# Convolution taps on one engine, tokens and context together, and two modulation groups in another stage

## The chip, the cores and the metric
The kernel runs on one core of a Trainium2 chip. The metric is the device time of one execution in microseconds. TensorE (PE) multiplies matrices, VectorE (DVE), ScalarE (ACT) and GpSimd (POOL) work on tiles of 128 partitions, and SyncE (SP) issues most transfers. Each engine executes its own queue of instructions in order.

## The reference
Two transformer blocks run one after the other on 512 tokens of width 1024 and, in the first block, 256 context tokens. The first block has two layers (`l` = 0 and 1). What matters for the change:

```python
def conformer_conv(u, conv_w, conv_b, ln_g, ln_b):
    a, gate = jnp.split(u, 2, axis=-1)
    h = a * jax.nn.sigmoid(gate)
    half = C_CONV_WIDTH // 2                       # C_CONV_WIDTH = 31
    h = lax.conv_general_dilated(h, conv_w[:, None, :], window_strides=(1,), padding=((half, half),),
                                 dimension_numbers=('NWC', 'WIO', 'NWC'),
                                 feature_group_count=C_CHANNELS) + conv_b   # C_CHANNELS = 256
    return jax.nn.silu(layer_norm(h, ln_g, ln_b))

# per layer: six modulation vectors of 1024 from the condition c (and from c_ctx for the context)
m = jax.nn.silu(cond) @ w_mod_l[:, :n_chunks * D_MODEL] + b_mod_l[:n_chunks * D_MODEL]
h = modulate(x, sh1, sc1)          # layer_norm(x) * (1 + sc1) + sh1
u = h @ w_in_l                     # queries, keys, values of attentions A and B, the convolution's 512 columns
x = layer_norm(DEEPNORM_ALPHA * x + g1 * o, ...)       # o: attentions and convolution through w_out
h2 = modulate(x, sh2, sc2)
x = layer_norm(DEEPNORM_ALPHA * x + g2 * ec_moe(h2, ...), ...)   # 16 experts
```

In layer 0 the convolution runs on the tokens and, apart from them, on the context; in layer 1 on the tokens alone. Only the shift and scale of the first LayerNorm (`sh1`, `sc1`) are needed before the projections; `g1`, `sh2`, `sc2` and `g2` are needed behind the attention.

## The kernel before
The stages follow one another: in layer 0 the LayerNorm and first modulation (to some 40 us), the projections with the convolution (to 245), attention (to 408), the output projection and router (to 500), the experts (to 1130); then layer 1 with its two LayerNorms (to 1190), projections (to 1313), attention (to 1420), output projection and experts; then the second block.

**Projections.** `gemm(j)` (L418) makes one of 16 chunks of 128 columns. The activations are split into `hi` and `lo` (HH, HL) and the weights into `wh` (cast on ACT, L300) and `wl` (the difference, L288, on DVE), so that three matmuls per k (128 rows) keep the precision; all matmuls go through the helper `mm`, L98. `px` holds 512 tokens, `pc` 256 context tokens. `wh` and `wl` have two buffers each: the cast for chunk j+2 waits for the last matmul of chunk j, and `wl` stands behind that in DVE's queue. Chunks 0 to 3 give the convolution's input `hp` (L492), 4 to 6 the keys, which `ksplit` (L444 to L451) splits through one buffer `kf` (filled by ACT, L459 and L460), 7 to 12 the queries, 13 to 15 the values. Chunk 4 and the queries of A are rotated (`rope`: a matmul into `rot`, `t` on DVE L439, `qf` times `cos` on POOL L440, the sum L441).

**Convolution.** For each of two groups of 128 channels, `hp` holds the tokens with 15 zeros on either side and behind them the context with its own zeros (`segs`). Tap 0 is a product plus bias on POOL (L504). The token taps are one DVE instruction each (L510), acc = hp shifted by t, times cw[t], plus acc, over 128x512. The context taps take two POOL instructions each over 128x256: a product into `cvt` (L516) and an addition to `acc` (L517). In layer 1, which has no context, the last 12 taps of each channel group go to POOL in the same manner over 128x512 (L520 to L524, `POOL_TAPS`), into an accumulator that DVE adds (L525). `taps(n)` issues the next n DVE taps between projections, and `conv_out` ends the convolution with LayerNorm and SiLU.

**Modulation.** `mod_group(l, g)` (L152) computes two of layer l's six vectors for both conditions: eight k-steps, each a load of 1 MB of `w_mod` through a ring of four buffers that the projection weights share (`load`, L144, issued by SP in order), and four matmuls with the columns `sT`; then a bias addition on DVE (`bm`, L160), a write of `ms` to memory, four transposes (L166) and copies into `modT` (L169). `mods` chains groups, and `next(mods)` advances by one k-step. Layer 0's projections work off (0,1) and (0,2), one step per `gemm`; layer 0's attention works off (1,0), (1,1) and (1,2), one step per unit. Layer 1 has none. `sT` is used again by the router (L753).

A scheduler of the language's compiler settles the order on each engine by its own estimates; `keep_in_program_order` pins a few instructions, so moving or resizing one instruction reorders its neighbours.

Of the kernel before, what the change touches and what calls it, by code (L numbers as in the profile page):

```python
# [10 lines left out]
F32 = mybir.dt.float32  # L11
# [3 lines left out]
AF = mybir.ActivationFunctionType  # L15
OP = mybir.AluOpType
# [4 lines left out]
P = 128  # L21
# [7 lines left out]
NEG = -1.0e30  # L29
RING = 4  # L30
MRING = (7, 9)
POOL_TAPS = (0, 12)
RIGHT = (1, 3)


# [26 lines left out]
class K:  # L62
# [38 lines left out]
    def setup(self):  # L101
        nc, A = self.nc, self.A
        self.cp = self.pool(self.es, "consts")
        self.ringp = self.pool(self.es, "ring", bufs=RING)
        self.dr = self.pool(self.es, "scratch", space=DRAM)
        self.ident = self.t(self.cp, [P, P], tag="ident")
        nc.scalar.dma_start(self.ident, A["ident"])
        self.nh8 = self.t(self.cp, [P, 8], tag="nh8")
        nc.gpsimd.memset(self.nh8, -0.5)
        self.nhalf = self.nh8[:, 0:1]  # L110
        cT = self.t(self.cp, [P, KC, 2], tag="cT")
        nc.scalar.dma_start(cT, A["cT"])
        self.sT = self.t(self.cp, [P, KC, 32], tag="sT")
        nc.gpsimd.memset(self.sT, 0.0)
        th = self.t(self.cp, [P, KC, 2], tag="cth")
        nc.scalar.activation(th, cT, AF.Tanh, scale=0.5)
        nc.vector.tensor_scalar_mul(cT, cT, 0.5)
        nc.vector.scalar_tensor_tensor(out=self.sT[:, :, 0:2], in0=th, scalar=1.0, in1=cT, op0=OP.add, op1=OP.mult)
        self.lnc = self.t(self.cp, [P, KC], tag="lnc")
        nc.gpsimd.dma_start(self.lnc, A["ln1_T"])  # L120
        self.xsum = [self.t(self.cp, [P, 1], tag=f"xsum{t}") for t in range(6)]
        self.modT = [self.t(self.cp, [P, 2, 48], tag=f"modT{l}") for l in range(2)]
        self.ms = {}

    def pipeline(self, units):

# [107 lines left out]
    def layer(self, l):  # L234
        nc, A, es = self.nc, self.A, ExitStack()
        last = l == 1
        NT = 4 if last else 6
        W = 512 if last else 768
# [15 lines left out]
        cw = self.t(kvp, [P, 2, 31], tag="cw")  # L254
# [3 lines left out]
        cb, cg5, cb5 = vec[:, 0, :], vec[:, 1, :], vec[:, 2, :]  # L258
# [18 lines left out]
        ps = self.pool(ea, f"psa{l}", bufs=2, space=PSUM)  # L277
# [8 lines left out]
        def low(j, eng):  # L286
            wt, wh, wl = nw[j]
            return eng.tensor_tensor(out=wl, in0=wt, in1=wh.bitcast(F32), op=OP.subtract)  # L288

        def weights(j, ahead=False):  # L290
            if j % 2 == 0:
                self.wt = self.load(A["w_in_t"][l, j // 2].rearrange("p k f -> p (k f)")).rearrange("p (k f) -> p k f", k=KC)
            wt = self.wt[:, :, (j % 2) * P : (j % 2) * P + P]
            if j in (2, 3):

                wh, wl = (kb[:, o * D : (o + 1) * D].rearrange("p (k f) -> p k f", k=KC) for o in (2 * j - 4, 2 * j - 3))
            else:
# [10 lines left out]
        if l == 0:  # L308

            zT = QA + QB + [vz[:, 0:768], vz[:, 768:1536]]  # L310
            for t in range(6):
                self.ln(XN[:, t, :], XN[:, t, :], small)
                for k0 in (0, 4):
                    tp = self.t(ps, [P, 4, P], tag="tr")
# [15 lines left out]
        else:  # L330

            gb = self.ring().rearrange("p (i d) -> p i d", i=2)
            for i in range(2):
                nc.sync.dma_start(gb[:, i], A["ln_vec"][l - 1, 2 + i : 3 + i, :].broadcast_to([P, D]))
            pin = self.tc.keep_in_program_order
            weights(0, ahead=True)
            weights(1, ahead=True)
            weights(2, ahead=True)
# [58 lines left out]
        ev = ExitStack()  # L397
        cvp = ev.enter_context(self.tc.tile_pool(name=f"conv{l}", bufs=1, side="right", reuse_waits="tile"))
        hp = [self.t(cvp, [P, W + (30 if last else 60)], tag=f"hp{c}") for c in range(2)]
        acc = [self.t(cvp, [P, W], tag=f"acc{c}") for c in range(2)]  # L400
        for c in range(2):
            nc.gpsimd.memset(hp[c][:, 0:15], 0.0)
            nc.gpsimd.memset(hp[c][:, 527:542], 0.0)
# [4 lines left out]
        wkp = self.pool(ea, f"wk{l}", bufs=2)  # L408
# [4 lines left out]
        nc.sync.dma_start(cos, A["cosA"])  # L413
        nc.sync.dma_start(sin, A["sinA"])

        mods = self.mods([(0, 1), (0, 2)] if l == 0 else [], ps, "mod", wkp, 1)

        def gemm(j, need_c):  # L418
            if len(nw) <= j:
# [63 lines left out]
        segs = [(0, 512, 15)] + ([] if last else [(512, 256, 557)])  # L483
        for c in range(2):
            px, pc = gemm(2 * c, not last)
            th = self.t(wkp, [P, 768], tag="kf", bufs=1)
# [6 lines left out]
        tap = []  # L493
# [4 lines left out]
            del tap[:n]  # L498

        def conv(c):  # L500
            for a, n, o in segs:
                o -= 15
                dst = acc[c][:, a : a + n]
                nc.gpsimd.tensor_scalar(dst, hp[c][:, o : o + n], cw[:, c, 0:1], cb[:, c : c + 1], op0=OP.mult, op1=OP.add)  # L504

                n0 = 31 if a else 31 - POOL_TAPS[l]
                for t in range(1, n0):
                    if a == 0:
                        tap.append(
                            lambda dst=dst, o=o, n=n, t=t: nc.vector.scalar_tensor_tensor(  # L510
                                out=dst, in0=hp[c][:, o + t : o + t + n], scalar=cw[:, c, t : t + 1], in1=dst, op0=OP.mult, op1=OP.add
                            )
                        )
                    else:
                        tmp = self.t(wkp, [P, 256], tag="cvt", bufs=4)
                        nc.gpsimd.tensor_scalar(tmp, hp[c][:, o + t : o + t + n], cw[:, c, t : t + 1], 0.0, op0=OP.mult, op1=OP.add)  # L516
                        nc.gpsimd.tensor_tensor(out=dst, in0=dst, in1=tmp, op=OP.add)  # L517
                if n0 < 31:
                    dst2 = self.t(cvp, [P, n], tag=f"acc2{c}")
                    for t in range(n0, 31):  # L520
                        tmp = dst2 if t == n0 else self.t(cvp, [P, n], tag="cvt2", bufs=2)
                        nc.gpsimd.tensor_scalar(tmp, hp[c][:, o + t : o + t + n], cw[:, c, t : t + 1], 0.0, op0=OP.mult, op1=OP.add)
                        if t > n0:
                            nc.gpsimd.tensor_tensor(out=dst2, in0=dst2, in1=tmp, op=OP.add)  # L524
                    tap.append(lambda dst=dst, dst2=dst2: nc.vector.tensor_tensor(dst, dst, dst2, op=OP.add))  # L525

        def conv_out():
            for t0, t1 in ((0, 4), (4, NT)):
                if t1 == t0:
                    continue  # L530
                zz = []
                for t in range(t0, t1):
                    tp = self.t(ps, [P, 512], tag="tr")
                    for c in range(2):
                        nc.tensor.transpose(tp[:, c * P : (c + 1) * P], acc[c][:, t * P : (t + 1) * P], self.ident)
                    mv, rs = self.ln_stats(tp, small, 256)
                    z = self.t(wkp, [P, 256], tag="cvt", bufs=4)
                    nc.vector.tensor_scalar(z, tp[:, 0:256], mv[:, 0:1], rs, op0=OP.subtract, op1=OP.mult)
                    zz.append(z)
                n, q0 = (t1 - t0) * P, t0 * P  # L540
                for c in range(2):
                    tp = self.t(ps, [P, 512], tag="tr")
                    for i, z in enumerate(zz):
                        nc.tensor.transpose(tp[:, i * P : (i + 1) * P], z[:, c * P : (c + 1) * P], self.ident)
                    u = self.t(wkp, [P, 512], tag="qf")
                    th = self.t(wkp, [P, 512], tag="t2")
                    nc.scalar.activation(u[:, :n], tp[:, :n], AF.Identity, bias=cb5[:, c : c + 1], scale=cg5[:, c : c + 1])
                    nc.scalar.activation(th[:, :n], u[:, :n], AF.Tanh)
                    nc.vector.scalar_tensor_tensor(out=acc[c][:, q0 : q0 + n], in0=th[:, :n], scalar=1.0, in1=u[:, :n], op0=OP.add, op1=OP.mult)

        for c in range(2):
            conv(c)
# [24 lines left out]
        MH = self.t(mixp, [P, KC, 768], F32R, tag="hi")  # L577
        ML = self.t(mixp, [P, KC, 768], F32R, tag="lo")
        self.MH, self.ML = MH, ML
        for c in range(2):  # L580
            nc.scalar.copy(MH[:, 6 + c, 0:W], acc[c])
            nc.vector.tensor_tensor(ML[:, 6 + c, 0:W], acc[c], MH[:, 6 + c, 0:W].bitcast(F32), op=OP.subtract)
        ea.close()
        ev.close()

# [2 lines left out]
        ap_ = self.pool(eb, f"at{l}", bufs=2)  # L588
        sm = self.pool(eb, f"ats{l}", bufs=4)
        ps = self.pool(eb, f"psb{l}", bufs=2, space=PSUM)  # L590
# [149 lines left out]
        ps = self.pool(ec, f"psc{l}", bufs=2, space=PSUM)  # L740
# [1246 lines left out]
```

## Time and profile before
| | us |
|---|---|
| median of 3 runs | 2653.32 (2651.34 to 2657.65) |
| profiled execution, its own time | 2650.53 |
| its span, first to last instruction | 2648.4 |
| TensorE busy | 2442.7 (92%) |
| VectorE / ScalarE / GpSimd busy | 1204.3 / 707.6 / 579.5 |
| mean granted TensorE clock | 0.964 |

The span leaves out 2.1 us around the first and the last instruction. Busy shares are means over stages with very different limits, so the rows below look at stages: how busy each engine is in a stretch of time, what an engine waited for, and single instructions in order of time. [...]

### The profile page before, as it was taken

How to read it: one execution, taken by the hardware profiler on the slowest of the kernel's cores; microseconds unless marked ns; L12 is line 12 of the kernel's file. 1: busy time of each engine (PE TensorE's matmuls, PEld its weight loads, DVE VectorE, ACT ScalarE, POOL GpSimd, SP SyncE). 2: the span in 40 equal slices, each digit the busy share in tenths (PEclk: the TensorE clock that was granted, in tenths of full speed). 3: DMA queues.
4: the chain of work that ended last, by engine and by line, in shares of the span. 5: the costliest groups of instructions: out<-in, count | busy, mean ns of one | idle time of the engine just before them, and what ended most of it. 6: DMA issues, size and time to landing. Idle time of an engine off the chain costs nothing. (4 is left out here: it accounts for less than half of the span.)

```text
span 2648.4 us, 37078 instructions
## 1 busy us (share of the span) xinstructions
PE 2442.7 (92%) x14946; PEld 1471.4 (56%) x14946; DVE 1204.3 (45%) x2478; ACT 707.6 (27%) x1404; POOL 579.5 (22%) x747
## 2 busy tenths in 40 slices
PE   6779999899999999957999699999989999999999
PEld 3566677533333333246787443333337878888887
DVE  6874675612222222379586412221138577432332
ACT  3023562210111110142364210000014357222321
POOL 4971350100000000069242100000005234111100
PEclk9989999899999999978999799999999999999999
DMA  8235804599999888530202699999992311222320
GB/s 341 95 119 211 301 22 152 207 358 409 352 335 340 337 328 334 207 125 32 80 25 105 244 419 420 420 419 420 420 395 84 125 49 52 85 96 80 112 96 32
DMA packets 141436, 581.42 MB, mean 220 GB/s; under 512 B 11985, under 2 KB 13009, under 8 KB 125649
## 3 DMA queue, kind: packets, MB, share of 16 engines
q1 hardware_dynamic: 132368, 549.62, 53.8%
q0 software_dynamic: 5152, 18.88, 1.9%
q10 hardware_dynamic: 3744, 10.56, 1.0%
q8 instruction: 117, 1.92, 0.3%
q14 instruction: 55, 0.44, 0.1%
HBM read 568.54 MB, written 10.49 MB: 219 GB/s over the span
## 5 line engine op out<-in xcount | busy, mean ns | idle before, releaser
L98 PE MATMUL mm<-m,xt 128*32 128x512 f32 (+1 forms) x2536 | 403.9, 594 | 0.0
L98 PEld LDWEIGHTS mm<-m,xt 128*32 128x32 f32 (+1 forms) x2536 | 119.3, 115 | 211.5 <-issue 205.0
L98 PE MATMUL mm<-r,xt 128*32 128x512 f32 (+1 forms) x1128 | 232.5, 595 | 0.0
L1153 DVE TENSOR_TENSOR xn<-xn,tr 128x512 f32<-128x512 f32 x120 | 78.4, 685 | 249.3 <-PE tr L98 249.3
L98 PE MATMUL mm<-m,hT 128*32 128x512 f32 (+1 forms) x792 | 179.8, 597 | 6.0 <-DMA m<-w_down 6.0
L978 POOL DMA_INDIRECT gat<-zd,ip x24 | 22.9, 954 | 623.1 <-PE tr L986 583.5
L98 PE MATMUL mm<-mr,xt 128*32 128x512 f32 (+1 forms) x432 | 131.4, 605 | 1.5 <-DVE xt L991 1.2
L510 DVE SCALAR_TENSOR_TENSOR acc<-hp,cw,acc 128x512 f32<-128x512 f32 x96 | 123.3, 1300 | 10.2 <-POOL acc L504 8.4
L98 PE MATMUL mm<-r,hT 128*32 128x512 f32 (+1 forms) x560 | 125.5, 597 | 1.9 <-DMA r<-w_down 1.9
L1120 DVE SCALAR_TENSOR_TENSOR yf<-mm,gp,g 128x512 f32<-128x512 f32 x32 | 24.0, 751 | 223.1 <-PE mm L98 221.4
L98 PEld LDWEIGHTS mm<-r,xt 128*32 128x32 f32 (+1 forms) x1128 | 67.4, 117 | 88.3 <-issue 83.5
L98 PE MATMUL px<-hi,wh 128*128 128x512 f32 x224 | 95.3, 431 | 18.9 <-ACT kf L459 17.2
L98 PE MATMUL px<-hi,wl 128*128 128x512 f32 x224 | 93.6, 418 | 20.5 <-DVE wl L288 20.5
L640 POOL TENSOR_SCALAR p<-p,rl 128x768 f32<-128x768 f32 (+2 forms) x96 | 79.1, 828 | 133.1 <-DVE rl L639 94.7
L98 PEld LDWEIGHTS mm<-m,hT 128*32 128x32 f32 (+1 forms) x792 | 52.9, 121 | 94.8 <-issue 73.6
L98 PE MATMUL pv<-ptT,VN 128*64 128x128 f32 x1360 | 95.4, 284 | 6.5 <-DVE lo L622 5.5
L98 PE MATMUL px<-HH,uh 128*128 128x512 f32 x256 | 99.9, 391 | 0.7 <-ACT HH L1777 0.7
L98 PE MATMUL po<-dl,rh 128*128 128x512 f32 x256 | 99.2, 390 | 1.4 <-DVE dl L1207 1.4
L98 PE MATMUL px<-HH,ul 128*128 128x512 f32 x256 | 99.9, 390 | 0.0
L98 PE MATMUL px<-HL,uh 128*128 128x512 f32 x256 | 99.9, 390 | 0.0
L98 PE MATMUL po<-dh,rh 128*128 128x512 f32 x256 | 98.9, 390 | 0.0
L98 PE MATMUL po<-dh,rl 128*128 128x512 f32 x256 | 98.6, 390 | 0.0
(523 smaller groups left out, 5326.1 us busy)
## 6 DMA issues: line engine op xcount, KB each, us to landing
m<-w_gate SPq DMA_DIRECT2D x79, 1024.0 KB, 14.6
m<-w_down SPq DMA_DIRECT2D x71, 1024.0 KB, 17.8
m<-w_up SPq DMA_DIRECT2D x62, 1024.0 KB, 9.5
r<-w_mod SPq DMA_DIRECT2D x48, 1024.0 KB, 6.4
r<-w_down SPq DMA_DIRECT2D x41, 1024.0 KB, 9.4
r<-w_up SPq DMA_DIRECT2D x40, 1024.0 KB, 17.8
r<-w_gate SPq DMA_DIRECT2D x31, 1024.0 KB, 13.2
mr<-w_up SPq DMA_DIRECT2D x20, 1024.0 KB, 5.2
```

The lines of the kernel that those rows point to most:

```text
L98: return self.nc.tensor.matmul(out, lhsT, rhs, start=start, stop=stop)
L510: lambda dst=dst, o=o, n=n, t=t: nc.vector.scalar_tensor_tensor(out=dst, in0=hp[c][:, o + t : o + t + n], scalar=cw[:, c, t : t + 1], in1= ...
L640: nc.gpsimd.tensor_scalar(p[:, :n], p[:, :n], rl, 0.0, op0=OP.mult, op1=OP.add)
L978: nc.gpsimd.indirect_dma_start(out=g[0:n], out_offset=None, in_=self.zd[l][s], in_offset=bass.IndirectOffsetOnAxis(ap=self.route[s][2][0:n ...
L1120: nc.vector.scalar_tensor_tensor(out=y, in0=d, scalar=gp[:, p : p + 1], in1=G2[0][:, c], op0=OP.mult, op1=OP.mult)
L1153: nc.vector.tensor_tensor(dst, dst, so, op=OP.add)
```

## The change
All 31 taps are computed without POOL. Tap 0 (product and bias) is an ACT instruction; the other 30 of each channel group are DVE instructions. In layer 0 one instruction covers tokens and context: `hp` is read over 798 = 512 + 30 + 256 elements, and `acc` has 30 unused columns between tokens and context (the context begins at `A0` = 542). Layer 1 has 60 DVE taps of 512 instead of 36 and two additions. The normalised values `z` use `hp`'s space in place of `cvt`, and the split of the convolution's result into MH and ML is made in one piece for tokens and one for context. The groups (1,1) and (1,2) move from layer 0's attention into layer 1's projections, so each layer's projections carry (l,1) and (l,2), and layer 0's attention carries (1,0) alone. As `sT` has been overwritten by then, `set_s` fills it again before layer 1.

```diff
-POOL_TAPS = (0, 12)
...
+    def set_s(self):
+        nc, (th, cT) = self.nc, self.silu
+        nc.gpsimd.memset(self.sT, 0.0)
+        nc.vector.scalar_tensor_tensor(out=self.sT[:, :, 0:2], in0=th, scalar=1.0, in1=cT, op0=OP.add, op1=OP.mult)
...
             pin = self.tc.keep_in_program_order
+            self.set_s()
             weights(0, ahead=True)
...
-        acc = [self.t(cvp, [P, W], tag=f"acc{c}") for c in range(2)]
+        acc = [self.t(cvp, [P, W if last else W + 30], tag=f"acc{c}") for c in range(2)]
+        A0 = 542
...
-        mods = self.mods([(0, 1), (0, 2)] if l == 0 else [], ps, "mod", wkp, 1)
+        mods = self.mods([(l, 1), (l, 2)], ps, "mod", wkp, 1)
...
         def conv(c):
-            for a, n, o in segs:
-                o -= 15
-                dst = acc[c][:, a : a + n]
-                nc.gpsimd.tensor_scalar(dst, hp[c][:, o : o + n], cw[:, c, 0:1], cb[:, c : c + 1], op0=OP.mult, op1=OP.add)
-                n0 = 31 if a else 31 - POOL_TAPS[l]
...
+            dst = acc[c]
+            n = dst.shape[1]
+            nc.scalar.activation(dst, hp[c][:, 0:n], AF.Identity, bias=cb[:, c : c + 1], scale=cw[:, c, 0:1])
+            for t in range(1, 31):
+                tap.append(
+                    lambda t=t: nc.vector.scalar_tensor_tensor(
+                        out=dst, in0=hp[c][:, t : t + n], scalar=cw[:, c, t : t + 1], in1=dst, op0=OP.mult, op1=OP.add
+                    )
+                )
...
-                    z = self.t(wkp, [P, 256], tag="cvt", bufs=4)
+                    z = hp[t % 2][:, t // 2 * 256 : t // 2 * 256 + 256]
...
         for c in range(2):
-            nc.scalar.copy(MH[:, 6 + c, 0:W], acc[c])
-            nc.vector.tensor_tensor(ML[:, 6 + c, 0:W], acc[c], MH[:, 6 + c, 0:W].bitcast(F32), op=OP.subtract)
+            for (a, n, o), q0 in zip(segs, (0, A0)):
+                nc.scalar.copy(MH[:, 6 + c, a : a + n], acc[c][:, q0 : q0 + n])
+                nc.vector.tensor_tensor(ML[:, 6 + c, a : a + n], acc[c][:, q0 : q0 + n], MH[:, 6 + c, a : a + n].bitcast(F32), op=OP.subtract)
...
-        mods = self.mods([(1, 0), (1, 1), (1, 2)] if l == 0 else [], ps, "mod", ap_, 1)
+        mods = self.mods([(1, 0)] if l == 0 else [], ps, "mod", ap_, 1)
```

The order of VectorE's queue in layer 0, from the first taps to the rotation of chunk 4, before. `hp_95` is the input of the second channel group, `wl_1058` the low half of chunk 6's weights:

```order
L510 SCALAR_TENSOR_TENSOR acc_96_433<-hp_94_431,cw_124,acc_96_433 128x512 x18
L492 SCALAR_TENSOR_TENSOR hp_95_432<-kf_632,px_643 128x512
L492 SCALAR_TENSOR_TENSOR hp_95_432<-kf_632,pc_644 128x256
L510 SCALAR_TENSOR_TENSOR acc_96_433<-hp_94_431,cw_124,acc_96_433 128x512 x3
L510 SCALAR_TENSOR_TENSOR acc_97_434<-hp_95_432,cw_124,acc_97_434 128x512
...
L288 TENSOR_TENSOR wl_1058<-r_1055,wh_1057 128x1024
...
L439 TENSOR_TENSOR t_189_956<-rot_954,sin_449 128x512
```

The same place in the changed kernel, where the same product is `wl_876`:

```order
L514 SCALAR_TENSOR_TENSOR acc_96_433<-hp_94_431,cw_124,acc_96_433 128x798 x13
L500 SCALAR_TENSOR_TENSOR hp_95_432<-kf_632,px_643 128x512
L500 SCALAR_TENSOR_TENSOR hp_95_432<-kf_632,pc_644 128x256
L514 SCALAR_TENSOR_TENSOR acc_96_433<-hp_94_431,cw_124,acc_96_433 128x798 x2
L514 SCALAR_TENSOR_TENSOR acc_97_434<-hp_95_432,cw_124,acc_97_434 128x798
...
L293 TENSOR_TENSOR wl_876<-r_873,wh_875 128x1024
...
L447 TENSOR_TENSOR t_129_774<-rot_772,sin_449 128x512
```

Taps of 798 elements stand in place of those of 512, and fewer of them ahead of each product: 13 instead of 18 ahead of the second `hp`, and counted from the first tap, 23 instead of 32 ahead of this `wl` and 31, 37, 41, 46 and 53 ahead of the next five (42, 46, 53 and twice 60 before).

PE's queue at the beginning of layer 1 in the changed kernel, from the last product of the experts to the transposes of the second LayerNorm (`VN`, `z`; `r` is a ring buffer with `w_mod`):

```order
L97 MATMUL tr_8553<-yc_1595_8509,oh_1592_8501 128x512
L97 MATMUL mod_8897<-r_8898,sT_69 32x512 x4
L97 MATMUL mod_8897<-r_8931,sT_69 32x512 x4
L97 MATMUL mod_8897<-r_8963,sT_69 32x512 x4
L375 MATMUL tr_8707<-ident_63,VN_8573 128x128
L375 MATMUL tr_8716<-ident_63,VN_8573 128x128
...
L97 MATMUL mod_8897<-r_8996,sT_69 32x512 x4
L375 MATMUL tr_8707<-ident_63,z_1666_8703 128x128
```

Before, the first of these transposes followed the last product of the experts at once. The other four steps of this group now stand among the remaining transposes and the first projections, and the second group's eight among the later projections.

SP's queue for the same stage in the changed kernel (the first two loads of `w_in_t`, the bias, band and table loads are left out; `x2d` is a write of the residual):

```order
L149 DMA r_8898<-w_mod 128x2048
L149 DMA r_8931<-w_mod 128x2048
...
L362 DMA x2d_92<-xn_3798 128x1024
L149 DMA r_8963<-w_mod 128x2048
...
L149 DMA r_9388<-w_mod 128x2048
L149 DMA r_9435<-w_in_t 128x2048
...
L168 DMA ms_1766_9338<-bm_8895 128x512
L157 DMA bm_9385<-bmr 128x512
L149 DMA r_9441<-w_mod 128x2048
```

Before, this queue held eight loads of `w_in_t` and no `w_mod`, `bm` or `ms`. Now loads of `w_mod` alternate with those of `w_in_t`, the third waits its turn behind the first `x2d`, and the second group's loads stand behind the write of `ms`.

## Rows read from the trace of the kernel before
**Rows 1.** The page, part 1: busy us, share of the span, instructions.
```profile
PE 2442.7 (92%) x14946; PEld 1471.4 (56%) x14946; DVE 1204.3 (45%) x2478; ACT 707.6 (27%) x1404; POOL 579.5 (22%) x747
```
**Rows 2.** Four stretches: length, busy PE, PEld, DVE, ACT, POOL, clock, DMA share, GB/s.
```profile
100.00:180.00 80.00, 50.51 (x254) 39.25 (x252) 79.45 (x57) 16.74 (x24) 77.23 (x89) 0.83 0.21 74
...
245.00:340.00 95.00, 88.13 (x726) 55.55 (x728) 66.50 (x204) 54.06 (x121) 35.22 (x52) 0.99 0.81 304
...
1190.00:1250.00 60.00, 46.86 (x195) 37.71 (x194) 59.17 (x49) 14.79 (x21) 59.45 (x42) 0.89 0.07 21
...
1320.00:1410.00 90.00, 84.25 (x822) 74.48 (x823) 74.21 (x209) 63.03 (x143) 45.24 (x77) 0.96 0.06 18
```
**Rows 3.** Waits, 60 to 225 us: engine, line, releaser: us, times, longest.
```profile
PE px L98 <- DVE wl L288: 13.0, 3, 10.8
...
PE px L98 <- ACT kf L459: 8.9, 1, 8.9
...
PE mod L166 <- DVE bm L160: 6.1, 1, 6.1
```
**Rows 4.** Stretches of 10 us in layer 0's projections.
```profile
110.00:120.00 10.00, 3.75 (x11) 3.22 (x12) 10.00 (x6) 0.00 (x0) 10.00 (x13) 0.51 0.01 2
...
130.00:140.00 10.00, 3.99 (x12) 3.48 (x13) 9.94 (x8) 4.82 (x7) 10.00 (x10) 0.53 0.20 55
...
150.00:160.00 10.00, 6.99 (x29) 6.14 (x30) 9.94 (x8) 2.65 (x4) 10.00 (x12) 0.66 0.17 54
```
**Rows 5.** Groups by shape, DVE, 0 to 420 us: busy us, mean ns | idle before.
```profile
L510 DVE SCALAR_TENSOR_TENSOR acc<-hp,cw,acc 128x512 f32<-128x512 f32 x60 | 76.8, 1300 | 8.5 <-POOL acc L504 7.4
...
L288 DVE TENSOR_TENSOR wl<-r,wh 128x1024 fp32r<-128x1024 f32 x14 | 21.4, 1544 | 8.0 <-ACT wh L300 8.0
```
**Rows 6.** Timeline of DVE: start us, duration us (layer 0; the last row layer 1).
```profile
67.81 17.55 DVE L510 SCALAR_TENSOR_TENSOR acc<-hp,cw,acc 128x512 f32<-128x512 f32 x18
...
130.84 0.73 DVE L510 SCALAR_TENSOR_TENSOR acc<-hp,cw,acc 128x512 f32<-128x512 f32 x1
...
135.87 1.21 DVE L288 TENSOR_TENSOR wl<-r,wh 128x1024 fp32r<-128x1024 f32 x1
...
1135.79 1.28 DVE L353 SCALAR_TENSOR_TENSOR xn<-xn,rs,r 128x1024 f32<-128x1024 f32 x1
```
**Rows 7.** Timeline of ACT: the casts behind projections 4, 9, 10 and 11.
```profile
92.72 1.05 ACT L300 CAST wh<-r 128x1024 fp32r<-128x1024 f32 x1 [18.22 <-PE pc L98]
...
177.03 1.05 ACT L300 CAST wh<-r 128x1024 fp32r<-128x1024 f32 x1 [11.18 <-PE pc L98]
...
188.46 1.05 ACT L300 CAST wh<-r 128x1024 fp32r<-128x1024 f32 x1 [9.61 <-PE pc L98]
...
198.96 1.05 ACT L300 CAST wh<-r 128x1024 fp32r<-128x1024 f32 x1 [8.68 <-PE pc L98]
```
**Rows 8.** Timeline of PE: one k-step of a modulation group.
```profile
103.47 1.07 PE L98 MATMUL mod<-r,sT 128*32 128x512 f32 x8
```
**Rows 9.** The tile `mod`, PE, 245 to 345 us: passes and waits.
```profile
L98 PE MATMUL mod<-r,sT x192: 590/592/617, 246.8 to 329.5; 128*32 128x512 f32 x192
...
  DMA r<-w_mod: 3.1, 2
```
**Rows 10.** Timeline, layer 1: PE's first transposes; SP's writes of `x2d`.
```profile
1144.23 0.69 PE L369 MATMUL tr<-ident,VN 128*128 128x128 f32 x2 [10.53 <-DVE VN L362]
...
1137.11 9.94 SPq L356 DMA_DIRECT2D x2d<-xn  x4
```
**Rows 11.** The page, part 6: loads of `w_mod`, KB each, us to landing.
```profile
r<-w_mod SPq DMA_DIRECT2D x48, 1024.0 KB, 6.4
```
**Rows 12.** Waits, 1120 to 1310 us (layer 1).
```profile
PE px L98 <- ACT kf L459: 8.3, 2, 7.1
...
PE px L98 <- DVE wl L288: 7.5, 2, 4.9
```
**Rows 13.** Groups by shape, DVE, 1120 to 1310 us.
```profile
L510 DVE SCALAR_TENSOR_TENSOR acc<-hp,cw,acc 128x512 f32<-128x512 f32 x36 | 46.5, 1300 | 1.7 <-POOL acc L504 1.0
```

More of the change, by code (lines that the diff above doesn't have):

```diff
@@ L113, in setup @@
         self.sT = self.t(self.cp, [P, KC, 32], tag="sT")
-        nc.gpsimd.memset(self.sT, 0.0)
         th = self.t(self.cp, [P, KC, 2], tag="cth")
@@ L117, in setup @@
         nc.vector.tensor_scalar_mul(cT, cT, 0.5)
-        nc.vector.scalar_tensor_tensor(out=self.sT[:, :, 0:2], in0=th, scalar=1.0, in1=cT, op0=OP.add, op1=OP.mult)
+        self.silu = th, cT
+        self.set_s()
         self.lnc = self.t(self.cp, [P, KC], tag="lnc")
@@ L335, in layer @@
             pin = self.tc.keep_in_program_order
+            self.set_s()
             weights(0, ahead=True)
@@ L500, in conv @@
         def conv(c):
-            for a, n, o in segs:
-                o -= 15
-                dst = acc[c][:, a : a + n]
-                nc.gpsimd.tensor_scalar(dst, hp[c][:, o : o + n], cw[:, c, 0:1], cb[:, c : c + 1], op0=OP.mult, op1=OP.add)
-                n0 = 31 if a else 31 - POOL_TAPS[l]
[L507 to L525, printed above, removed]
+            dst = acc[c]
[7 more added lines that the diff above has]
+                )
         def conv_out():
@@ L531, in conv_out @@
                 zz = []
+                n, q0 = (t1 - t0) * P, (A0 if t0 else 0)
                 for t in range(t0, t1):
@@ L534, in conv_out @@
                     for c in range(2):
-                        nc.tensor.transpose(tp[:, c * P : (c + 1) * P], acc[c][:, t * P : (t + 1) * P], self.ident)
+                        nc.tensor.transpose(tp[:, c * P : (c + 1) * P], acc[c][:, q0 + (t - t0) * P : q0 + (t - t0 + 1) * P], self.ident)
                     mv, rs = self.ln_stats(tp, small, 256)
-                    z = self.t(wkp, [P, 256], tag="cvt", bufs=4)
+                    z = hp[t % 2][:, t // 2 * 256 : t // 2 * 256 + 256]
                     nc.vector.tensor_scalar(z, tp[:, 0:256], mv[:, 0:1], rs, op0=OP.subtract, op1=OP.mult)
                     zz.append(z)
-                n, q0 = (t1 - t0) * P, t0 * P
                 for c in range(2):
```

## The prediction, made before the changed kernel ran
> **What bounds the kernel now.** I read the page's first part, then the table of stretches, then what each engine waits for, then single instructions. On the page TensorE is busy 92% of the span, VectorE 45%, GpSimd 22% [rows 1]: on average TensorE decides, and work taken off the others is worth nothing. The table of stretches shows where that fails [rows 2]: from 100 to 180 us (layer 0's projections while the convolution runs) PE is busy 50.51 of 80 us while VectorE is busy 79.45 and GpSimd 77.23, and layer 1's projections repeat it (46.86 of 60 us against 59.17 and 59.45). In both stretches of attention PE is busy over 92% of the time. The convolution therefore matters only in the two projection stages; in attention only PE's own work counts.
>
> The waits name the late work [rows 3]. From 60 to 225 us PE waits 13.0 us for `wl` (L288, the low half of the next projection's weights), 8.9 us for `kf` (L459, on ACT, behind VectorE's key split) and 6.1 us for `bm` (L160): 28.0 of the 29.5 us that PE stands idle from 100 to 180. All three producers sit in VectorE's one queue, between taps. The stalls have a second price: in three of these slices the granted clock is 0.51, 0.53 and 0.66 [rows 4], after slices with long PE gaps. The full clock would have needed 3.75 x 0.49 + 3.99 x 0.47 + 6.99 x 0.34 = 6.1 us less for the same busy time.
>
> **The taps' price.** The 60 taps cost 1300 ns each and `wl` 1544 ns on average [rows 5], with GpSimd full beside them [rows 2]; isolated ones cost 0.73 and 1.21 us [rows 6]. No row shows a tap of 798 elements. Below, the bound is a tap of 512 (0.73). The same operation over 1024 elements takes 1.28 us [rows 6]. On the line between, 0.73 + 286 x 0.55 / 512 = 1.04 us, which I take. Above, 798 elements at the contended mean: 1.30 x 798 / 512 = 2.03 us; I leave that to a rival, because GpSimd's 120 operations are gone.
> [...]
>
> **Layer 0's projections.** Sixty taps cost 60 x 1.04 = 62 us instead of 76.8, and the 8.5 us that they waited for their starting value [rows 5] shrink, since ACT, busy 16.74 of 80 us [rows 2], now writes it. The order moves too: `wl` stands behind 23, 31, 37, 41, 46 and 53 taps instead of 32, 42, 46, 53 and 60. I walked the queue with the uncontended prices. The 18 taps that start at 67.81 [rows 6] become 13, over at 81. The second `hp` waits for its projection, to about 84. Ten more taps and 1.21 put the first `wl` at 96, where PE wants it at 105. For the third, another 14 taps (14.6) with two `wl`, the key splits and the rotation (some 11.5) give 122; PE, at the 9.5 us per projection below, wants it at 124. Later ones come out 2 to 7 us early. So PE should run through with a margin of 2 us at its tightest. ACT's casts give a second way to the same sum [rows 7]: they follow each projection, 10.50 us apart once the taps are over (about 9.5 without the rotation), but 84.3 us lie between the ends of the projections 4 and 9, where four of 9.5 and one of 10.5 need 48.5; excess 36. All of it is 29.5 + 6.1 = 35.6. As the margin is thin I leave 5 us of stalls: -31 (from -20, if half the margins fail, to -36).
>
> **Layer 0's attention.** Two groups leave it. A k-step is eight recorded passes and takes 1.07 us [rows 8]; 24 (192 passes) stand here in three groups [rows 9], so 16 x 1.07 is 17 us of PE work, the transposes not counted. PE is busy 88.13 of 95 us there, and 84.25 of 90 in layer 1's attention, which has no such steps [rows 2]: so taking them out does not open new gaps, though the clock may drop from 0.99 to that stretch's 0.96, some 2 us. Up to 3.1 us of waits for `w_mod` [rows 9] may go as well. -16 (-10 to -21).
>
> **Layer 1.** The same 17 us come back here. Half lies in a hole: PE sits idle 10.53 us before the first LayerNorm transposes at 1144.23 [rows 10]. Three k-steps now stand ahead of those in PE's queue; the third one's load stands behind the x2d write at 1137.11 on SP [rows 10] and lands some 6.4 us later [rows 11], at 1143.5, so its 1 to 2 us at the low clock may delay the transposes by as much. The other eight k-steps with the transposes, 9.5 us, come among the projections, where PE now waits 8.3 + 7.5 us [rows 12] and loses 46.86 x 0.11 = 5.2 us to the clock [rows 2]. VectorE gets 24 taps more, but 60 x 0.73 = 44 us is less than today's 36 x 1.30 = 46.8 [rows 13]. So 21 us could go and 11 come; with 4 us of stalls left, -6 (-13, if the steps keep the clock up too, to +10, if no stall goes and the added steps lie open). `set_s` adds one memset on GpSimd and one small VectorE operation in the expert stage, where GpSimd is idle; the memset precedes gathers of `gat`. Nothing. The split copies (four pieces instead of two) add under 1 us at the stage's end.
>
> The expert stages and the second block do not change; they shift. Sum: -31 - 16 - 6 = -53 on the profiled 2650.5 us. On the median of the runs shown, 2653.3, 2.8 us above it, this gives 2600 us.
>
> **The rivals.**
> 1. **Half of it comes back as waits.** VectorE has one queue, and PE still waits for `wl` and for the key splits in it. Against this: the walk above; for it: a margin of 2 us over six weights, and in layer 1 no idle VectorE at all (59.17 of 60). If layer 0 gives 18, attention 12 and layer 1 costs 3: 2653 - 27 = 2626. Chance 0.22.
> 2. **Loads of w_mod stall PE in layer 1 (slower).** There 16 loads of 1 MB enter a ring of four buffers, in SP's order, between w_in loads that wait until VectorE has made `wl`, behind a write of `ms` that waits for VectorE's `bm`. PE executes in order, so each late k-step holds the projection behind it. A load takes 6.4 us to land [rows 11]. At a wait of 5.5 us for each of 16 steps: +88 - 53, about 2688. It decides at 53 / 16 = 3.3 us each. Against it: the same steps in layer 0 show no wait for a load among those of [rows 3]; in layer 1 the DMA share is only 0.07 [rows 2]. Chance 0.04.
> 3. **VectorE is saturated, and more work on it makes it worse (slower).** If the tap's price is its own and not GpSimd's, it is 2.03 us: layer 0's taps cost 122 us instead of 76.8, layer 1's 60 x 1.30 = 78 instead of 46.8. Then +45 - 8 in layer 0 and +25 in layer 1 against -16: 2653 + 46 = 2699. The 0.73 us of an isolated tap [rows 6] speaks against it. Chance 0.02. [...]
> 4. **It does not do what it says.** The order shows the steps and taps moved, so this could only be that the gains cancel: 2653. Chance 0.03.
>
> **How the numbers follow.** The forecast has 0.69. The range runs from near the sum's favourable ends (-36 - 19 - 13 = -68, 2585) to rival 1 and a little beyond, 2632. Outside are rivals 2 to 4 and the tails. About 0.2% (5 us) can be told from no change. Faster by more: forecast and rival 1, 0.91; within it, rival 4, 0.03; slower, rivals 2 and 3, 0.06.
>
> **What would show it.** Right: taps of about 1.04 us in layer 0 and 0.73 in layer 1; PE idle below 6 us in the stretch that takes the place of 100 to 180, with a clock near 1; ACT's casts 9.5 to 10.5 us apart throughout; attention 16 us shorter; the expert stage starting some 47 us sooner. Wrong: PE waiting for `wl`, `kf` or, in layer 1, for `r<-w_mod`; taps above 1.3 us with GpSimd quiet; attention's PE idle share grown from 7% to over 15%.

## The result, and the profile after

The changed kernel takes 2587.6 us (median of 4 runs, 2586.2 to 2587.6) against 2652.8 us (4 runs) before: ratio 0.975, 95% interval 0.9733 to 0.9767, so 65 us faster. The forecast was 2600 us with a range of 2585 to 2632. The profiled executions differ by 2650.53 - 2587.57 = 63.0 us. The page's first part, after (compare [rows 1]; in the views a name such as `px<-hi,wl` reads output from inputs, 128x512 is partitions by elements, and a granted clock of 1.00 is the full one):

```profile
PE 2432.4 (94%) x14946; PEld 1459.7 (56%) x14946; DVE 1162.1 (45%) x2503; ACT 710.6 (27%) x1410; POOL 400.6 (15%) x576
```

PE's busy time fell by 10.3 us (2442.7 before); the other 52 us of the shorter span were idle time. The tiles `px` (projections) and `pv` (attention) mark the stages. Rows of the tile view from 45 us on, before, for layer 0, layer 1 and attention (durations, then first and last start):

```profile
L98 PE MATMUL px<-hi,wl x111: 388/397/796, 44.9 to 242.4; 128*128 128x512 f32 x111
...
L98 PE MATMUL px<-lo,wh x112: 387/394/793, 1159.4 to 1307.7; 128*128 128x512 f32 x112
...
L98 PE MATMUL pv<-ptT,VN x576: 272/273/476, 263.1 to 407.3; 128*64 128x128 f32 x192
```

The same after:

```profile
L97 PE MATMUL px<-hi,wl x111: 388/397/628, 44.9 to 204.3; 128*128 128x512 f32 x111
...
L97 PE MATMUL px<-lo,wh x112: 388/394/793, 1109.9 to 1246.0; 128*128 128x512 f32 x112
...
L97 PE MATMUL pv<-ptT,VN x576: 272/273/476, 224.6 to 355.4; 128*64 128x128 f32 x192
```

| stage, between these marks | before | after | change | forecast |
|---|---|---|---|---|
| layer 0's projections (44.9 to the last `px`) | 197.5 | 159.4 | -38.1 | -31 |
| layer 0's attention (to the last `pv`) | 164.9 | 151.1 | -13.8 | -16 |
| output, experts, layer 1's LayerNorms (to `px` of layer 1) | 752.1 | 754.5 | +2.4 | about +1 |
| layer 1's projections | 148.3 | 136.1 | -12.2 | -7 |
| the rest of the span | 1340.7 | 1339.8 | -0.9 | 0 |

The forecast gave -6 for the third and fourth rows together; the split between them is read from its terms. The first row begins where the view does: the projections' first `px` stood at 40.1 us before and at 38.9 after, so 1.2 of the 38.1 us lie ahead of them, and from first to last `px` they take 165.4 us instead of 202.3.

In layer 0 the stalls are gone: from 60 to 210 us PE waits 0.2 us in all. ACT's casts behind projections 4, 5, 9 and 10, after [rows 7]:

```profile
91.62 1.05 ACT L305 CAST wh<-r 128x1024 fp32r<-128x1024 f32 x1 [7.27 <-PE pc L97]
102.07 1.05 ACT L305 CAST wh<-r 128x1024 fp32r<-128x1024 f32 x1 [8.65 <-PE pc L97]
...
139.93 1.05 ACT L305 CAST wh<-r 128x1024 fp32r<-128x1024 f32 x1 [7.84 <-PE pc L97]
150.43 1.05 ACT L305 CAST wh<-r 128x1024 fp32r<-128x1024 f32 x1 [8.68 <-PE pc L97]
```

From 91.62 to 139.93 are 48.3 us where 84.3 stood, and 48.5 was the pace without a stall. The taps and `wl` in VectorE's groups from 0 to 420 us, and below them layer 1's taps from 1070 to 1250 us [rows 5, 13], each with count, busy time and mean ns:

```profile
L514 DVE SCALAR_TENSOR_TENSOR acc<-hp,cw,acc 128x798 f32<-128x798 f32 x60 | 62.1, 1063 | 0.9
...
L293 DVE TENSOR_TENSOR wl<-r,wh 128x1024 fp32r<-128x1024 f32 x14 | 16.9, 1217 | 7.5 <-ACT wh L305 7.5
```

```profile
L514 DVE SCALAR_TENSOR_TENSOR acc<-hp,cw,acc 128x512 f32<-128x512 f32 x60 | 44.1, 762 | 1.7 <-ACT acc L511 1.0
```

A tap of 798 takes 1.063 us (forecast 1.04). The stretches, after [rows 2]: layer 0's projections, its attention, layer 1's projections (columns as there):

```profile
100.00:140.00 40.00, 40.00 (x234) 32.18 (x232) 37.61 (x42) 15.04 (x22) 0.00 (x0) 1.00 0.43 145
...
205.00:356.00 151.00, 134.98 (x1246) 107.87 (x1239) 111.63 (x350) 97.87 (x241) 62.98 (x122) 0.95 0.19 74
...
1138.00:1186.00 48.00, 47.38 (x234) 36.92 (x234) 44.70 (x64) 17.13 (x24) 4.29 (x4) 1.00 0.41 150
```

PE is full at the full clock while VectorE is still busy 37.61 of 40 us: it was not relieved of much, it was on time. How early shows at the tightest `wl`, behind 37 taps: ready at 116.97, and wanted by PE 5.7 us later.

```profile
115.76 1.21 DVE L293 TENSOR_TENSOR wl<-r,wh 128x1024 fp32r<-128x1024 f32 x1
...
122.65 0.40 PE L97 MATMUL px<-hi,wl 128*128 128x512 f32 x1
```

### The profile page after: what moved, and what is told of

It is laid out like the page before. It is cut to its first block, busy times and chain, and to the rows that moved or that the text cites. A ratio compares the mean times of both kernels' runs of the same rounds, so it can differ in the third digit from the quotient of the medians.

```text
span 2585.8 us, 36931 instructions
## 1 busy us (share of the span) xinstructions
PE 2432.4 (94%) x14946; PEld 1459.7 (56%) x14946; DVE 1162.1 (45%) x2503; ACT 710.6 (27%) x1410; POOL 400.6 (15%) x576
## 3 DMA queue, kind: packets, MB, share of 16 engines
q8 instruction: 117, 1.92, 0.3%
## 5 line engine op out<-in xcount | busy, mean ns | idle before, releaser
L514 DVE SCALAR_TENSOR_TENSOR acc<-hp,cw,acc 128x798 f32<-128x798 f32 (+1 forms) x120 | 106.2, 912 | 2.6 <-ACT acc L511 1.0
L1087 ACT COPY hT<-tr 128x512 f32<-128x512 f32 x16 | 9.4, 587 | 330.5 <-PE tr L1086 330.5
L984 DVE TENSOR_SCALAR xt<-tr,modT 128x128 f32<-128x128 f32 (+1 forms) x96 | 35.9, 388 | 131.8 <-ACT xt L986 130.8
## 6 DMA issues: line engine op xcount, KB each, us to landing
mr<-w_up SPq DMA_DIRECT2D x20, 1024.0 KB, 18.2
```

The costliest lines, as they stand in the source:

```text
L514: lambda t=t: nc.vector.scalar_tensor_tensor(out=dst, in0=hp[c][:, t : t + n], scalar=cw[:, c, t : t + 1], in1=dst, op0=OP.mult, op1=OP.add)
L984: nc.vector.tensor_scalar(o, i, sc, sh, op0=OP.mult, op1=OP.add)
L1087: (nc.vector.tensor_copy if k0 else nc.scalar.copy)(ht[:, k0 : k0 + 4, :].rearrange("p k s -> p (k s)"), tp)
```

## The experiments

**The two parts apart.** `e1_conv_alone` keeps the modulation's lists as before, `e2_mods_alone` keeps the convolution as before:

```diff
# e1, on the changed kernel (and no set_s before layer 1)
-mods = self.mods([(l, 1), (l, 2)], ps, "mod", wkp, 1)
+mods = self.mods([(0, 1), (0, 2)] if l == 0 else [], ps, "mod", wkp, 1)
...
-mods = self.mods([(1, 0)] if l == 0 else [], ps, "mod", ap_, 1)
+mods = self.mods([(1, 0), (1, 1), (1, 2)] if l == 0 else [], ps, "mod", ap_, 1)
# e2: the same two lines the other way round on the kernel before, with set_s
```

> All of the convolution's change, none of the modulation's: (1,1) and (1,2) stay in layer 0's attention. Theory A (the stalls in both projection stages went because VectorE was freed; the moved steps cost as much PE time in layer 1's projections as they freed in attention, but for those in the hole before the LayerNorm): layer 0's projections 38 us shorter as in the changed kernel, attention unchanged, layer 1's projections some 20 us shorter; 2588 to 2597 us, near 2591, so the move of the groups is worth only 0 to 6 us. Theory B (the two parts add as in the prediction, the move is worth 10 or more): 2600 us or above.

> The modulation's move alone, the convolution as before, with GpSimd's taps. Attention 14 us shorter in every theory. Theory A (layer 1's stalls behind VectorE stay, and the eight steps among the projections run inside them): layer 1 longer by 0 to 6 us, 2638 to 2646 us. Theory B (each step costs its PE time): layer 1 longer by 11, about 2650 us. Theory C (rival 2: the loads of w_mod wait in the ring behind w_in buffers that VectorE frees late): over 2655 us, with PE waiting for r<-w_mod by 10 us or more.

Measured: 2599.4 us (ratio 0.979, 0.978 to 0.981) and 2639.8 us (0.995, 0.993 to 0.997), beside 2654.4 us before: -55 and -14.6, together -70 where both at once give -65. So the parts nearly add. For e1, 2599.4 lies between the two theories: the move is worth 12 us on top of the convolution, more than A gave it. For e2 A holds, at the end of its range: layer 1's projections, from first to last `px`, grow by 6.0 us (149.7 to 155.7), less than the steps' own time, since the steps run in part inside stalls that are there anyway. Why the steps cost so little in layer 1 stands in one stretch of e1, the same place as the last row above:

```profile
1154.00:1202.00 48.00, 43.71 (x202) 35.72 (x201) 43.56 (x59) 17.24 (x24) 4.29 (x4) 0.96 0.11 35
```

Without the steps PE is idle 4.3 of 48 us and its clock is at 0.96; with them it is idle 0.6 us at 1.00. They fill gaps, and the clock stays up in this stretch.

**Joining tokens and context.** `e3_two_instructions` splits each tap of layer 0 again, both halves on VectorE:

```diff
-out=dst, in0=hp[c][:, t : t + n], ...
+for (_, m, _), q0 in zip(segs, (0, A0)):
+    out=dst[:, q0 : q0 + m], in0=hp[c][:, q0 + t : q0 + t + m], ...
```

> The changed kernel, but each tap of layer 0 is two VectorE instructions, 512 for the tokens and 256 for the context. Theory A (freeing GpSimd is what helped; joining matters little): a pair costs some 1.05 to 1.15 us, PE keeps running, 2587 to 2592 us. Theory B (joining is needed, because the margin of the queue is some 2 us): VectorE's taps 70 us or more instead of 62, stalls for wl return, 2595 us or above.

Measured: 2588.5 us (0.975, 0.973 to 0.976), A's range, but with the taps that B expected:

```profile
L516 DVE SCALAR_TENSOR_TENSOR acc<-hp,cw,acc 128x512 f32<-128x512 f32 x60 | 45.1, 752 | 0.0
...
L516 DVE SCALAR_TENSOR_TENSOR acc<-hp,cw,acc 128x256 f32<-128x256 f32 x60 | 29.2, 487 | 0.0
```

That is 74.3 us instead of 62.1, nearly the 76.8 of the kernel before, and PE waits no longer than in the changed kernel. One instruction instead of two is worth nothing measurable here, and the sum of the taps' time alone does not make the stalls.

**GpSimd beside the taps.** `e4_pool_beside` gives GpSimd the old operations back, on a buffer `spare` that nothing reads:

```diff
 tap.append(...)
+if not last:
+    ...
+    nc.gpsimd.tensor_scalar(tmp, hp[c][:, A0 + t : A0 + t + 256], cw[:, c, t : t + 1], 0.0, op0=OP.mult, op1=OP.add)
+    nc.gpsimd.tensor_tensor(out=spare, in0=spare, in1=tmp, op=OP.add)
```

> The changed kernel, and in layer 0 GpSimd does the old context taps again (60 products and 60 additions over 256 elements), into a buffer that nothing reads, so the result is the same. VectorE's order and operations are those of the changed kernel. Theory A (GpSimd's reads hold up VectorE's taps): the taps rise from 1.06 us to 1.5 to 2.0, wl from 1.2 to 1.5 or more, the stalls come back, 2610 to 2640 us. Theory B (the gain is from the queue's new order and from tap 0 on ACT, not from the contention): taps stay near 1.1 us, 2588 us.

Measured: 2631.0 us (0.991, 0.989 to 0.992), 43 us lost. This is in A's range, but not by A's means: the taps rose only to 1.24 us. The waits from 60 to 240 us:

```profile
DVE QA L450 <- POOL qf L449: 29.7, 3, 28.4
PE px L97 <- DVE wl L293: 20.2, 1, 20.2
PE px L97 <- ACT kf L468: 17.7, 1, 17.7
DVE kf L450 <- POOL qf L449: 13.7, 1, 13.7
```

The rotation's product stood behind the extra work in GpSimd's queue, and VectorE's queue stood behind that. To take this away, `e5_control` puts the product on VectorE (`nc.vector.tensor_tensor(qf, qf, cos, op=OP.mult)`), `e5_beside` adds e4's operations to it, `e8_beside_short` only those with `t < 24`, so that GpSimd is free when the LayerNorm of `conv_out` needs it.

> The changed kernel with one move: the rotation's product with cos is on VectorE instead of GpSimd, so GpSimd has nothing in the projections that anybody waits for but the LayerNorms' rs. It is the control for the next two. Five instructions of 0.69 us more on VectorE in each layer, near the keys: 2587 to 2590 us in every theory; over 2592 would say that VectorE's queue has no margin.

> The control, and beside the taps of layer 0 GpSimd's 120 old operations into a buffer that nothing reads. In the run with them before, VectorE waited 13.7 and 28.4 us for the rotation's product, which stood behind them in GpSimd's queue; here it can't. Theory A (contention for SBUF reads alone costs what the change gained): taps at 1.3 us, so the third wl is late by some 8 us and stalls of 8 to 20 us return, 2596 to 2610 us. Theory B (GpSimd's queue was the harm): taps may be slower, but PE runs through, 2587 to 2592 us.

> The control with the rotation's product on VectorE, and GpSimd's reading operations beside only the first 23 taps of each channel group (92 instead of 120), so that its queue is empty before the convolution's LayerNorm needs its rs; in the run with all 120 PE lost 17.9 us there. What is left is the contention alone, in the changed kernel's order. Theory A (contention alone explains the 36 us that layer 0's projections lost before): stalls of 25 us or more, over 2612 us. Theory B (with the new order of the queue a contended tap costs only the thin margins): casts as in the run with 120, 7 us late, 2593 to 2598 us.

Measured: 2588.3, 2614.8 (0.985, 0.983 to 0.986) and 2597.9 us (0.979, 0.977 to 0.980). The control changes nothing. e5_beside is slower than either theory said: PE lost 17.9 us waiting for `hp` at `conv_out`, behind `rs` in GpSimd's queue. In e8 that is gone (1.0 us is left), and what remains is the contention: taps of 1.27 us, and PE's wait for one late copy. Its groups from 0 to 420 us, and its waits from 60 to 270:

```profile
L517 DVE SCALAR_TENSOR_TENSOR acc<-hp,cw,acc 128x798 f32<-128x798 f32 x60 | 74.9, 1273 | 0.9
```

```profile
PE px L97 <- ACT kf L468: 5.1, 1, 5.1
```

It costs 2597.9 - 2588.3 = 9.6 us, as B expected (5.8 between the profiled executions). So in the changed order, contention of this strength is not yet 36 us. But it is weaker than it was: a tap rose by 0.23 us here (1.045 in the control), and by some 0.54 in the kernel before (1.300, against 0.762 for 512 elements with GpSimd quiet). Is it the order, then?

**The old order.** `e10_old_order` holds layer 0's taps and `wl` in nearly the old order with GpSimd quiet:

```diff
-    f()
+    self.tc.keep_in_program_order(f())
...
-    low(j, nc.vector)
+    self.tc.keep_in_program_order(low(j, nc.vector))
...
+weights(4); weights(5); taps(32)    # ahead of projection 4, and other counts behind it
```

> The changed kernel, GpSimd quiet, with layer 0's taps and wl held in an order close to the one before: wl behind 28, 42, 46, 53 and 60 taps (32, 42, 46, 53 and 60 before; 23, 31, 37, 41 and 46 in the changed kernel). Theory A (the tap's price decides): stalls up to 12 us, 2588 to 2600 us. Theory B (the order decides): stalls of 20 us or more, 2608 us or above.

Measured: 2645.5 us (0.996, 0.995 to 0.998). The time lies in B's range, but it settles nothing: PE waited only 10.3 us for `wl`, while the pinning also moved PE's own order, and PE waited 15.8 us for `r<-w_mod` in layer 0's projections, which it does not in either kernel. The next run keeps both old orders almost as they are. `e11_old_memsets` is the kernel before with GpSimd's context taps replaced by memsets, so it leaves the context's convolution out:

```diff
-nc.gpsimd.tensor_scalar(tmp, hp[c][:, o + t : o + t + n], cw[:, c, t : t + 1], 0.0, op0=OP.mult, op1=OP.add)
-nc.gpsimd.tensor_tensor(out=dst, in0=dst, in1=tmp, op=OP.add)
+for _ in range(4):
+    nc.gpsimd.memset(dst, 0.0)
```

> The kernel before, in VectorE's and PE's old order (wl behind 32, 42, 47, 53 and 60 taps of 512), but in layer 0 GpSimd's 120 reading operations of the context taps are replaced by 240 memsets of the context's accumulator, so the context's convolution is left out. Theory A (before, contention decided, in whatever order): taps near 0.73 us, layer 0's projections 28 to 38 us shorter, 2615 to 2628 us. Theory B (the old order alone, with more taps ahead of wl, costs most of it): 2640 us or above.

Measured: 2633.0 us (0.993, 0.990 to 0.995), between the two. The timeline of VectorE says why, first before (the first 18 taps stand in [rows 6]), then in e11:

```profile
86.21 2.78 DVE L510 SCALAR_TENSOR_TENSOR acc<-hp,cw,acc 128x512 f32<-128x512 f32 x3
96.36 16.49 DVE L510 SCALAR_TENSOR_TENSOR acc<-hp,cw,acc 128x512 f32<-128x512 f32 x11 [7.38 <-POOL acc L504]
112.78 3.41 DVE L288 TENSOR_TENSOR wl<-r,wh 128x1024 fp32r<-128x1024 f32 x1
```

```profile
67.01 14.35 DVE L510 SCALAR_TENSOR_TENSOR acc<-hp,cw,acc 128x512 f32<-128x512 f32 x18
...
83.47 0.75 DVE L510 SCALAR_TENSOR_TENSOR acc<-hp,cw,acc 128x512 f32<-128x512 f32 x1
85.11 9.01 DVE L510 SCALAR_TENSOR_TENSOR acc<-hp,cw,acc 128x512 f32<-128x512 f32 x13 [0.90 <-POOL acc L504]
94.04 1.21 DVE L288 TENSOR_TENSOR wl<-r,wh 128x1024 fp32r<-128x1024 f32 x1
...
102.81 24.22 DVE L446 CAST KHA<-kf 64x768 fp32r<-64x768 f32 x1
126.95 0.73 DVE L510 SCALAR_TENSOR_TENSOR acc<-hp,cw,acc 128x512 f32<-128x512 f32 x1
```

The 60 taps take 0.762 us on average, the longest 1.20, and `wl`, behind 32 of them as before, is ready at 95 instead of 116: the taps were hardly held up. But one cast, 0.54 us in the changed kernel, took 24.22 us beside the memsets, and PE waited 17.0 us behind it. That is the whole loss of layer 0: ACT's casts behind projections 4 and 9 stand at 91.87 and 159.71, 67.8 us apart instead of 48.3, and one gap of theirs, 102.50 to 133.21, exceeds the pace of 10.5 us by 20. The others show no stall. By the marks of the first table layer 0's projections take 179.3 us in e11 and 161.1 in e1, layer 1's (which e11 leaves as before) 146.8 and 132.4. The two differences, 18.2 and 14.4, make up the 2631.4 - 2599.0 = 32.4 us between the profiled executions. So A holds for the taps: in the old order, too, they would not have stalled PE had GpSimd not held them up.

`e7_memsets` asks the same in the changed kernel: 120 memsets of 768 elements, and a product at the head of each group, beside the control's taps.

> The control, and beside the taps GpSimd fills a buffer 120 times (memsets of 768 elements, some 0.7 us each, 84 us in all; two products at their head read hp), which writes SBUF and reads nothing. [...] Theory B (any GpSimd access to SBUF holds them up): taps of 1.2 us or more and 2594 us or above.

Measured: 2590.8 us (0.976, 0.974 to 0.977), below B's 2594, and without B's taps of 1.2 us or more:

```profile
L517 DVE SCALAR_TENSOR_TENSOR acc<-hp,cw,acc 128x798 f32<-128x798 f32 x60 | 61.4, 1051 | 0.9
...
L523 POOL MEMSET spare<- 128x768 f32 x120 | 89.8, 748 | 6.9
```

So beside memsets a tap took 1.051 us, against 1.045 without them (e5_control) and 1.273 beside GpSimd's products and additions (e8). A cast beside memsets, on the other hand, took 24.22 us in e11. But the same casts in e7, beside memsets too, took 0.55 to 1.09 us (0.54 in the changed kernel):

```profile
106.79 0.55 DVE L455 CAST KHA<-kf 64x768 fp32r<-64x768 f32 x1
...
121.86 1.09 DVE L455 CAST kb<-kf 64x768 fp32r<-64x768 f32 x1
```

So a cast beside memsets is not always held for long; the last section comes back to it.

**One wait less.** `e9_tap0_act` is the kernel before with tap 0 on ACT:

```diff
-nc.gpsimd.tensor_scalar(dst, hp[c][:, o : o + n], cw[:, c, 0:1], cb[:, c : c + 1], op0=OP.mult, op1=OP.add)
+nc.scalar.activation(dst, hp[c][:, o : o + n], AF.Identity, bias=cb[:, c : c + 1], scale=cw[:, c, 0:1])
```

> The kernel before, with tap 0 alone moved from GpSimd to ACT, so that VectorE no longer waits 7.4 us for the second group's start behind GpSimd's context taps; wl stays behind 32, 42, 47, 53 and 60 taps. Theory A (that wait was part of the loss): layer 0's projections 5 to 8 us shorter, about 2645 us. Theory B (VectorE is late by so much, and GpSimd slows it for as long as its own taps last, that the wait only moves): 2650 us or above.

Measured: 2671.0 us (1.006, 1.004 to 1.008): slower than before, in B's range. VectorE's wait of 7.4 us is gone, but then one tap took 53 us, and PE waited 47.7 us for the `wl` behind it. The timeline, and the taps of layer 0 from 84 to 153 us (min, median, max):

```profile
85.80 65.67 DVE L510 SCALAR_TENSOR_TENSOR acc<-hp,cw,acc 128x512 f32<-128x512 f32 x14
151.39 1.21 DVE L288 TENSOR_TENSOR wl<-r,wh 128x1024 fp32r<-128x1024 f32 x1
```

```profile
L510 DVE SCALAR_TENSOR_TENSOR acc<-hp,cw,acc x16: 737/1037/53072, 83.8 to 152.5; 128x512 f32<-128x512 f32 x16
```

GpSimd's own operations meanwhile took 0.47 and 0.71 us, where they had taken 0.92 and 1.17 from 86 to 93 us, beside taps that went through. Its timeline:

```profile
126.91 0.47 POOL L516 TENSOR_SCALAR cvt<-hp,cw 128x256 f32<-128x256 f32 x1
127.36 0.71 POOL L517 TENSOR_TENSOR acc<-acc,cvt 128x256 f32<-128x256 f32 x1
```

So the price of contention is no constant: beside the same two operations of GpSimd one tap takes 1.04 us and another 53. What decides between the two no row shows.

**Layer 1's loads.** In the changed kernel PE waits for the third k-step's load ahead of layer 1's transposes. PE and SP there:

```profile
1093.57 1.93 PE L97 MATMUL mod<-r,sT 128*32 128x512 f32 x8 [8.47 <-DMA r<-w_mod]
```

```profile
1086.65 0.33 SPq L362 DMA_DIRECT2D x2d<-xn  x1
1087.08 0.37 SPq L149 DMA_DIRECT2D r<-w_mod  x1
```

`e6_x2d_pool` issues the writes of `x2d` from GpSimd: `nc.gpsimd.dma_start(self.x2d[...], x)`.

> The changed kernel, with the four writes of x2d in layer 1's transition issued by GpSimd instead of SP, so that the third and fourth loads of w_mod no longer stand behind them. Theory A (SP's order made PE wait 8.5 us for the third k-step, and that delayed the first LayerNorm transposes): k-steps three and four run in the hole, the transposes start 1.5 to 2 us sooner, 2583 to 2586 us. Theory B (the load waits for a free ring buffer or the hole is bound by VectorE's affine steps in any case, or GpSimd's issue delays rs): 2587 us or above.

Measured: 2593.2 us (0.977, 0.976 to 0.978), 5.6 us slower than the changed kernel, so in B's range. The trace shows something of both theories. The first two steps and the third, in the changed kernel (the third as above) and in e6, and e6's two loads:

```profile
1083.18 1.92 PE L97 MATMUL mod<-r,sT 128*32 128x512 f32 x16
```

```profile
1084.18 3.64 PE L97 MATMUL mod<-r,sT 128*32 128x512 f32 x16
1091.10 1.93 PE L97 MATMUL mod<-r,sT 128*32 128x512 f32 x8 [3.27 <-DMA r<-w_mod]
```

```profile
1086.17 2.04 SPq L149 DMA_DIRECT2D r<-w_mod  x2
```

In e6 the load waits for a ring buffer, as B has it: the first step, which frees one, starts at 1084.18, 1.0 us later than in the changed kernel, and the first two steps take 3.64 us instead of 1.92; at the third step's 1.93 us it ends at 1086.1, just ahead of the load at 1086.17. In the changed kernel the first step ended at 1084.2, so by the same order of loads a buffer was free 2.8 us before the load went out at 1087.08: there the write ahead of it did hold it, as A has it. And PE reaches the first transposes 26.5 us after the experts' last products instead of 28.0. What makes e6 slower stands behind them: PE then waits 9.2 us for `z`, since in GpSimd's new order `rs` stands behind 4.64 us of work on `kb`. What the load alone is worth stays open.

No version beat the changed kernel: e3 and the control are level with it.

## Why the prediction was right, and where its sizes were off

- What bounds: right. The gain came from the stages where PE stood idle behind VectorE, and from PE work that left attention.
- The taps' price: 1.04 us forecast, 1.063 measured; layer 1's 0.73, measured 0.762.
- Layer 0's projections: mechanism right, the term too small. It said "I leave 5 us of stalls: -31"; 0.2 us was left. 36.0 of the 38.1 us lie between the casts of projections 4 and 9, where 35.6 were given as the end of the range; 1.1 lie ahead of projection 4's cast, where the stage's earlier start has them already, and 1.0 behind projection 9's. The walk ("PE should run through with a margin of 2 us at its tightest") was right that PE runs through, but the margin was larger: 5.7 us at the same `wl`, and e3's 12 us more of taps cost nothing.
- Attention: -16 forecast, -13.8 measured. PE's work fell by 152.90 - 134.98 = 17.9 us, but the claim that this "does not open new gaps" failed by 4 us: idle time grew from 12.1 of 165 to 16.0 of 151 us, and the clock fell from 0.99 to 0.95. The largest growth is in PE's waits for VectorE's `m`, 7.0 us after and 2.0 before. The stretch before:

```profile
243.00:408.00 165.00, 152.90 (x1382) 109.02 (x1375) 113.85 (x355) 99.20 (x239) 63.64 (x122) 0.99 0.47 176
```

- Layer 1: -6 forecast for the transition and the projections together, -9.8 measured (+2.4 and -12.2). e1 has the convolution's part alone: by the same marks its projections take 132.4 us, 15.9 less than before, close to the 21 less 4 us of stalls that were forecast. Too large was "11 come". It put eight k-steps and the transposes, 9.5 us, among the projections; in fact twelve of the sixteen ran there, some 14 us of PE's work (row below), and yet the projections are only 136.1 - 132.4 = 3.7 us longer than in e1, since the steps fill gaps. "Half lies in a hole" was wrong in the same way: three steps stand in that hole. The delay of 1 to 2 us ahead of the transposes came about, 28.0 us after the experts' last products instead of 26.1, but 1.4 of it was made up on the way to the first `px`. The +2.4 of the table is for the most part the expert stage, in which nothing changed: 606.3 us before, 607.8 after, 608.2 in e1. The steps from 1108 to 1247 us (PE, PEld, DVE):

```profile
1108.00:1247.00 139.00, 14.15 (x96) 2.84 (x100) 0.94 (x3) 0.99 0.43 155
```

- Rival 1 (half comes back) did not happen. Rival 2 (w_mod's loads stall layer 1) shows in a single wait of 8.5 us, in a hole where PE had nothing else. Rival 3's price, 2.03 us for a contended tap of 798, was wrong: with GpSimd busy it is 1.24 to 1.27 us in three runs.
- The reason behind the contended price is the part of the prediction that needs a correction. It took 1.30 us as what GpSimd costs a tap. That is a mean over very unlike phases: 17.55 / 18 = 0.98 us in the first row of [rows 6], 1.67 in the tap at 137.01 of the same timeline, and 53 us once in e9. Also GpSimd's queue was not counted as a cost of its own: e4 and e5_beside lose 18 to 38 us of PE's time through products and `rs` that stand behind GpSimd's taps. The change removes both dangers at once. How the 36 us of layer 0 divide between these two was not measured: e11 shows that the old order alone loses nothing beyond one cast, e8 that contended taps in the new order lose 10. For the first and longest stall the two timelines above give an estimate. PE waited 10.8 us for a `wl` that was ready 20.9 us later than in e11; some 6.5 of these are VectorE's wait for a tap 0 that stood in GpSimd's queue (7.38 and 0.90), and some 15 the longer taps and the longer `wl` itself. A kernel in the old order with contended taps and the products off GpSimd was not tried, and layer 1's 15.9 us were not taken apart by a run of their own.

## What to carry to other kernels

Where VectorE is late for TensorE, look at what GpSimd does beside it before moving more work there. Here a pair of taps on VectorE with GpSimd quiet (0.752 + 0.487 us in e3) cost no more than the longer one of them beside a busy GpSimd (1.300 us before). Work without an urgent reader (here modulation steps) can go into a stage where PE has gaps: here some 14 us of it cost 4. Price the stall out completely if a walk of the queue says so, and bound the sum by the idle time that the row shows.

## What the runs showed of the hardware that was not expected

In two runs one VectorE instruction lasted as long as many of GpSimd's in a row. In e9 one tap of 512 elements took 53.07 us, while GpSimd ran some 90 operations of 0.47 and 0.71 us; it ended as GpSimd's series came to its last three additions. In e11 one cast took 24.22 us beside back-to-back memsets. In both, GpSimd was busy without a pause until just before the held instruction ended. The stretches of e9 (the tap ended at 149.2) and of e11 (the cast ended at 127.0):

```profile
99.00:148.00 49.00, 5.96 (x36) 4.05 (x34) 49.00 (x1) 0.00 (x0) 49.00 (x86) 0.60 0.06 21
148.00:150.00 2.00, 0.00 (x0) 0.00 (x0) 2.00 (x2) 0.00 (x0) 1.84 (x3) 0.50 0.00 0
```

```profile
104.00:126.00 22.00, 9.34 (x56) 7.16 (x54) 22.00 (x1) 0.41 (x1) 22.00 (x88) 0.83 0.14 48
126.00:128.00 2.00, 0.00 (x0) 0.00 (x0) 1.97 (x3) 0.83 (x1) 1.83 (x6) 0.50 0.00 0
```

In e7 GpSimd stood idle for 6.9 us in all before its 120 memsets, and it was busy for 1.89 of the 2 us of the row below, in which the cast at 106.79 took 0.55 us:

```profile
106.00:108.00 2.00, 2.00 (x13) 1.73 (x12) 1.97 (x3) 1.58 (x3) 1.89 (x3) 1.00 0.68 164
```

That a pause of GpSimd's lets the instruction through fits all three, but is a guess that was not tried, and it is not the whole of it: in the kernel before GpSimd was busy for 10.00 of the 10 us from 110 to 120 [rows 4], and no tap took longer than 1.77 us.
